# Attention of a four-layer trunk on one core: from one pair of heads at a time to groups of two pairs

## The chip, the cores and the metric

The kernel runs on one core of a Trainium2 chip. The metric is device time in microseconds (us) of one execution. Five engines work beside each other, each in the order of its own queue, and wait for each other by semaphores: PE (TensorE, matmuls and transposes into PSUM), DVE (VectorE), ACT (ScalarE), POOL (GpSimd) and SP, which issues DMAs.

## The reference, cut to what matters

A trunk of one block-sparse attention layer, which at 256 positions is plain causal attention of 16 heads, and one sliding-window layer of 16 query heads on 4 shared key/value heads with a learned sink in the denominator. Each is followed by an output projection and a gated FFN with a convolution over time.

```python
def reference(x, positions, ...):
    for l in range(DEPTH):                       # DEPTH = 2, SEQ = 256, D_MODEL = 1024
        h = rmsnorm(x, attn_norm[l])
        if l < N_A:                              # layer 0: q, k, v of 16 heads of 64
            q, k, v = jnp.split(h @ w_qkv_a[l], 3, axis=-1)
            ...
            o = moba_attention(to_bhsd(q), to_bhsd(k), to_bhsd(heads(v, N_HEADS)))
        else:                                    # layer 1: window of 128, sinks, 4 kv heads
            ...
            o = swa_sink_attention(to_bhsd(q), shared_k, shared_v, sinks_b[i])
        x = x + o.transpose(0, 2, 1, 3).reshape(B_, S_, N_HEADS * HEAD_DIM) @ w_o
        x = x + conv_ffn(rmsnorm(x, ffn_norm[l]), w_up[l], conv_w[l], conv_b[l], w_down[l])
    return rmsnorm(x, final_norm)
```

## The kernel before, in words

Every product in the weights goes as three fp32r matmuls on a high and a low part of each factor (hi·hi, hi·lo, lo·hi). ACT makes the high part of a weight unit (`wh`, L157), DVE the low part (`wl`, L160); a unit is 128x2048 and four are held at once, so the fifth may be written only after PE has read the first for the last time.

Attention takes the 16 heads as 8 pairs. For pair j:

- `score(j)`: three matmuls (L401 to L403) give the first 128 queries of both heads from a block-diagonal key tile `kd`, on all 128 rows of the array. Then six matmuls (L407) of 64 rows each give the second 128 queries, head e from rows 64e to 64e+63; the two heads of a pair can run side by side.
- softmax of each head: `masked` (DVE, L416), `exps` (ACT, L426, with a sink L429), `norm` (DVE L435, L437, L444 and ACT L442). It needs no PE.
- `probs_T(j)`: six transposes (L456), copied from PSUM by DVE (L464) and ACT (L462).
- `values(j)`: four fp32 matmuls (L477) that write 64 columns of the array each, again two heads side by side; each is recorded twice, once for each of two passes. The result is copied as a high part by ACT (L483) and a low part by DVE (L484) into the tile that the output projection reads.

Between these pieces `fill(ns)` takes other PE work from `filler`: the projections of the next q and k groups (L317 to L319) and, at the end, units of the output projection `Down` (L524, L525, L529). `Down` has four units of weights; unit i reads the values of pairs 2i and 2i+1. Two of its units are in the filler, the other two are done by `finish`, by blocks of 128 positions b and halves of the features n; `add` brings each (b, n) into the residual `xr`, and `feats` transposes it (L264) for the FFN, whose first matmuls are L612 to L614.

PSUM has eight banks under three tags: four `acc`, two `u`, two `t`. Steps off PE are put off with `chain` on a clock of estimated PE time. From `manual.close()` on, that is from the first score on, a scheduler of the framework decides the order on each engine from dependencies and priorities, so neighbouring pieces are interleaved there.

In this text a stretch is a run of PE instructions in one shape of the array: *full* (128 rows, 128 columns: projections, L401 to L403, transposes), *row* (64 rows, L407) or *column* (64 columns, L477).

Of the kernel before, what the change touches and what calls it, by code (L numbers as in the profile page):

```python
# [60 lines left out]
def trunk(ctx: ExitStack, tc, x, xw, pos, cpk, fin, sinks, w, out):  # L61
# [32 lines left out]
    def f(ap):  # L94
        return ap.bitcast(F32)

    def blk(b):
        return slice(b * P, (b + 1) * P)
# [279 lines left out]
    def attention(qk, ready, filler, lead, rate, msk, vcol, sink):  # L378

        oT = []  # L380
        budget = [0.0]
# [8 lines left out]

        def score(j):
            g, p = divmod(j, 2)
            while g not in qk:
                next(filler)
            require("qk", g)
            qh, ql, kh_, kl_, kcol, diag = qk[g]
            kc = kcol(p)
            dh, dl = diag(p)
            sa, sb = bank("u"), bank("u")
            o = sa[:, :S]  # L400
            nc.tensor.matmul(o, qh[:, p, blk(0)], dh, start=True, stop=False)  # L401
            nc.tensor.matmul(o, qh[:, p, blk(0)], dl, start=False, stop=False)
            nc.tensor.matmul(o, ql[:, p, blk(0)], dh, start=False, stop=True)  # L403
            for k, (q_, k_) in enumerate(((qh, kh_), (qh, kl_), (ql, kh_))):
                for e, o in enumerate((sa[:, S:], sb[:, :S])):
                    r = slice(e * HD, (e + 1) * HD)
                    nc.tensor.matmul(o, q_[r, p, blk(1)], k_[r, kc], start=(k == 0), stop=(k == 2))  # L407
            tick(640)
            pr = [row3() for _ in range(2)]
            st = wk.tile([P, 4, 4], F32, tag="hst", name=nm("hst"), bufs=4)  # L410

            def masked(e):
                h = 2 * j + e
                src = (sa[:, e * P:(e + 1) * P], sb[:, :S] if e else sa[:, S:])
                for qb in range(NB):
                    nc.vector.tensor_tensor_reduce(out=pr[e][:, qb * P:3 * P] if qb else pr[e][:, :P], in0=src[qb],  # L416
                                                   in1=msk if qb else msk[:, P:], scale=-0.125,
                                                   scalar=nsink[:, h:h + 1] if sink else 3e38, op0=ALU.add, op1=ALU.min,
                                                   accum_out=st[:, 0, 2 * e + qb:2 * e + qb + 1])
# [25 lines left out]

            chain(("sm", j), (200.0, lambda: masked(0)), (400.0, lambda: exps(0)), (600.0, lambda: norm(0)))
            chain(("sm", j), (300.0, lambda: masked(1)), (600.0, lambda: exps(1)), (600.0, lambda: norm(1)))
            return pr

# [19 lines left out]

        def values(j, pT):  # L470

            require("pT", j)
            ov = bank("t")[:, :S]
            for kb in range(NB):
                for e in range(2):
                    o = ov[e * HD:(e + 1) * HD]
                    nc.tensor.matmul(o[:, P:] if kb else o, v_sb[kb][:, vcol(2 * j + e)], pT[e][:, S:] if kb else pT[e][:, :S],  # L477
                                     start=(kb == 0), stop=(kb == 1))
            tick(640)
            if j % 2 == 0:  # L480
                pend[0] = quad()
            hi, lo = pend[0][:, j % 2], pend[0][:, 2 + j % 2]
            chain(("o", j // 2), (200.0, lambda: nc.scalar.activation(hi, ov, AF.Copy)),  # L483
                  (400.0, lambda: nc.vector.tensor_tensor(out=lo, in0=ov, in1=f(hi), op=ALU.subtract)))  # L484
            oT.append((hi, lo))

        ready(oT)
        state, pend = {}, [None]

        fill(lead)  # L490
        manual.close()
        state[0] = score(0)
        n_p = NH // 2
        for j in range(n_p):
            if j + 1 < n_p:
                state[j + 1] = score(j + 1)
            fill(rate(j) * 0.5)
            state[j] = probs_T(j, state[j])
            fill(rate(j) * (1-0.5))
            values(j, state.pop(j))  # L500
        for _ in filler:
# [3 lines left out]
    class Down:  # L505
# [33 lines left out]

        def finish(self, i0, after, tail=None):  # L540

# [5 lines left out]

            for b in range(NB):
                for n in range(2):
# [333 lines left out]
    def filler_a():  # L883
        yield from qk_group(1, U_QK[1])
        yield from qk_group(2, U_QK[2])
        yield from v_half(1, U_V1)
        yield from qk_group(3, U_QK[3])
        yield from o_down[0].units(0, 2)

    def ready_a(oT):  # L890
        o_down.append(Down(U_OA, 4, oT, lambda i: require("o", i)))

    attention(qk, ready_a, filler_a(), 8000.0, lambda h: 7500.0 if h < 6 else 5000.0, mask, lambda h: h, False)
    nc.gpsimd.affine_select(out=mask[:, :P], in_=mask[:, :P], compare_op=ALU.is_gt, fill=NEG, base=0,
# [10 lines left out]

    o_down[0].finish(2, after_a)
    kT_h = new_hT()
# [41 lines left out]
    def filler_b():  # L949
        for g in range(1, 4):  # L950
            yield from q_group(g)
        yield from o_down[0].units(0, 2)

    def ready_b(oT):
        o_down.append(Down(U_OB, 4, oT, lambda i: require("o", i)))

    attention(qk, ready_b, filler_b(), 5500.0, lambda h: 3000.0 if h<4 else 700.0, mask, lambda h: 2 * (h // 8) + h % 2, True)

# [8 lines left out]

    o_down[0].finish(2, after_b)

# [133 lines left out]
```

## Time and profile before

| | |
|---|---|
| median of 3 runs | 585.7 us (585.28 to 585.92) |
| profiled execution, its own time | 585.75 us |
| its span, first to last instruction | 583.8 us |
| PE busy / PEld busy | 574.1 us / 507.1 us |
| DVE / ACT / POOL busy | 432.2 / 381.8 / 105.7 us |
| DMA | 100.99 MB, mean 173 GB/s |

About 2 us of the time lie outside the span. PE is recorded busy nearly all the time; its matmuls overlap, so the distance from the start of one matmul to the start of the next tells more than busy time does. PEld is the loading of the stationary operand, which can run beside a matmul.

### The profile page before, as it was taken

The numbers are of one execution on the slowest core, as the hardware profiler recorded it, in microseconds if no ns is written. First come the engines' busy times: TensorE is split into PE (matmuls) and PEld (weight loads), VectorE is DVE, ScalarE is ACT, GpSimd is POOL, SyncE is SP. The second block draws the span as 40 slices with busy tenths as digits, with TensorE's granted clock in tenths as the row PEclk, the third lists the DMA queues.
The fourth block names the chain that finished last, engine by engine and source line by source line (L and its number), as shares of the span: only waits on it lengthen the run. The fifth ranks groups of instructions, "written<-read, shape, count | busy, mean of one in ns | idle before, by whom it ended". The sixth has DMA issues, their size and how long they took to land.

```text
span 583.8 us, 10178 instructions
## 1 busy us (share of the span) xinstructions
PE 574.1 (98%) x3858; PEld 507.1 (87%) x3858; DVE 432.2 (74%) x929; ACT 381.8 (65%) x768; POOL 105.7 (18%) x124
## 2 busy tenths in 40 slices
PE   8999999999999999999999999999999999999995
PEld 7877777789999999988888977679999999988884
DVE  6697667589977777677569778669987676777814
ACT  6888777579566565666459588758765665656513
POOL 7241001011222322221003000000222223232003
PEclk9999999999999999999999999999999999999999
DMA  8964334314654454547744522143364535446701
GB/s 326 359 265 145 145 144 149 140 60 158 217 198 165 168 194 148 204 153 291 285 144 153 209 74 74 72 145 145 120 241 154 209 145 190 172 163 234 288 0 72
DMA packets 15455, 100.99 MB, mean 173 GB/s; under 512 B 1968, under 2 KB 2096, under 8 KB 3888
## 3 DMA queue, kind: packets, MB, share of 16 engines
q1 hardware_dynamic: 15120, 100.09, 47.0%
q8 instruction: 30, 0.49, 0.3%
q10 hardware_dynamic: 288, 0.26, 0.1%
q14 instruction: 17, 0.14, 0.1%
HBM read 99.30 MB, written 1.05 MB: 172 GB/s over the span
## 4 chain that ended last, share of the span: by engine, by line
PE 60%; DVE 15%; ACT 8%; POOL 6%; issue 5%; DMA 3%; POOLq 0%; SPq 0%; DVEq 0%; ACTq 0%
PE acc L524 9%; PE acc L529 9%; PE acc L525 9%; POOL m L656 6%; DVE m L651 4%; DVE m L649 4%; DVE wl L160 4%; PE acc L317 4%; PE acc L318 4%; PE acc L319 3%; ACT m L645 3%; PE t L477 3%; DMA wr<-in_w 3%; PE t L456 2%; PE u L407 2%
## 5 line engine op out<-in xcount | busy, mean ns | idle before, releaser
L160 DVE TENSOR_TENSOR wl<-wr,wh 128x1024 fp32r<-128x1024 f32 (+1 forms) x200 | 218.9, 1115 | 32.5 <-ACT wh L157 32.2
L157 ACT ACTIVATE wh<-wr 128x1024 fp32r<-128x1024 f32 (+1 forms) x200 | 187.9, 971 | 30.8 <-PE acc L529 17.9
L656 POOL TENSOR_TENSOR m<-m,m 128x256 f32<-128x256 f32 x44 | 66.3, 1507 | 206.7 <-DVE m L651 178.2
L524 PE MATMUL acc<-wh,q 128*128 128x512 f32 x238 | 94.4, 397 | 0.0
L525 PE MATMUL acc<-wl,q 128*128 128x512 f32 x238 | 92.9, 390 | 0.0
L612 PE MATMUL u<-q,wh 128*128 128x256 f32 x320 | 88.4, 277 | 0.0
L613 PE MATMUL u<-q,wh 128*128 128x256 f32 x320 | 88.0, 275 | 0.0
L614 PE MATMUL u<-q,wl 128*128 128x256 f32 x320 | 88.0, 275 | 0.0
L612 PE MATMUL t<-q,wh 128*128 128x256 f32 x288 | 79.4, 276 | 0.7 <-DVE m L651 0.7
L613 PE MATMUL t<-q,wh 128*128 128x256 f32 x288 | 79.2, 275 | 0.0
L614 PE MATMUL t<-q,wl 128*128 128x256 f32 x288 | 79.2, 275 | 0.0
L529 PE MATMUL acc<-wh,q 128*128 128x512 f32 x238 | 79.0, 392 | 0.0
L660 ACT ACTIVATE q<-m 128x256 fp32r<-128x256 f32 x44 | 18.4, 418 | 81.4 <-POOL m L656 81.4
L613 PEld LDWEIGHTS u<-q,wh 128*128 128x128 f32 x320 | 60.1, 188 | 0.0
L614 PEld LDWEIGHTS u<-q,wl 128*128 128x128 f32 x320 | 60.1, 188 | 0.0
L612 PEld LDWEIGHTS u<-q,wh 128*128 128x128 f32 x320 | 59.9, 188 | 0.2
L317 PE MATMUL acc<-wh,q 128*128 128x512 f32 (+1 forms) x160 | 57.2, 358 | 0.0
L318 PE MATMUL acc<-wl,q 128*128 128x512 f32 (+1 forms) x160 | 56.0, 350 | 0.0
L319 PE MATMUL acc<-wh,q 128*128 128x512 f32 (+1 forms) x160 | 55.9, 349 | 0.0
L612 PEld LDWEIGHTS t<-q,wh 128*128 128x128 f32 x288 | 54.1, 188 | 1.0 <-ACT wh L157 0.5
L613 PEld LDWEIGHTS t<-q,wh 128*128 128x128 f32 x288 | 54.1, 188 | 0.0
L614 PEld LDWEIGHTS t<-q,wl 128*128 128x128 f32 x288 | 54.0, 188 | 0.0
(156 smaller groups left out, 1040.3 us busy)
## 6 DMA issues: line engine op xcount, KB each, us to landing
wr<-in_w SPq DMA_DIRECT2D x90, 1024.0 KB, 4.8
first<-in_xw SPq DMA_DIRECT2D x5, 384.0 KB, 5.7
xr<-in_x SPq DMA_DIRECT2D x2, 512.0 KB, 8.6
first<-in_xw SPq DMA_DIRECT2D x1, 768.0 KB, 7.1
out<-m SPq DMA_DIRECT2D x3, 256.0 KB, 2.1
fin_t<-in_fin SPq DMA_DIRECT2D x1, 512.0 KB, 5.7
first<-in_xw SPq DMA_DIRECT2D x1, 388.0 KB, 3.5
out<-m ACTq DMA_DIRECT2D x1, 256.0 KB, 2.1
```

The source lines that it names most:

```text
L157: nc.scalar.activation(wq[i][0][:, c], raws[i][:, c], AF.Copy)
L160: nc.vector.tensor_tensor(out=wq[i][1][:, c], in0=raws[i][:, c], in1=f(wq[i][0][:, c]), op=ALU.subtract)
L317: nc.tensor.matmul(o, xh[:, blk(b)], wh, start=(c == 0), stop=False)
L318: nc.tensor.matmul(o, xh[:, blk(b)], wl, start=False, stop=False)
L319: nc.tensor.matmul(o, xl[:, blk(b)], wh, start=False, stop=(c == KC - 1))
L524: nc.tensor.matmul(o, ph[:, blk(b)], hi[:, s_], start=first, stop=False)
L525: nc.tensor.matmul(o, ph[:, blk(b)], lo[:, s_], start=False, stop=False)
L529: nc.tensor.matmul(o, pl[:, blk(b)], hi[:, s_], start=False, stop=end)
L612: nc.tensor.matmul(o, hi[:, s_], xh, start=(c == 0), stop=False)
L613: nc.tensor.matmul(o, hi[:, s_], xl, start=False, stop=False)
L614: nc.tensor.matmul(o, lo[:, s_], xh, start=False, stop=(c == KC - 1))
L656: nc.gpsimd.tensor_tensor(out=h, in0=gs, in1=t[1], op=ALU.mult)
```

## The change: groups of two pairs

`score(j)` becomes `scores(g)`, which makes the scores of pairs 2g and 2g+1: six block-diagonal matmuls into a bank of their own (tag `acc`, or `t` once `Down` holds all four `acc`), then twelve row matmuls into the two `u` banks. `values(g)` does both pairs of a group into one `t` bank and copies it with one ACT and one DVE instruction of 512 columns. The loop emits `values(g)` right behind `scores(g + 1)`. Three of the four units of `Down` are now in the filler, and `finish` does the last one with the feature half outside and the position block inside (`by_half`). The leads and fill rates are new numbers, and the four heads of a group start their softmax 700 ns apart on the estimated clock.

```diff
-        def score(j):
-            g, p = divmod(j, 2)
+        def scores(g):
             ...
-            sa, sb = bank("u"), bank("u")
-            o = sa[:, :S]
-            nc.tensor.matmul(o, qh[:, p, blk(0)], dh, start=True, stop=False)
...
+            sd, sa, sb = bank("t" if o_down[0].acc else "acc"), bank("u"), bank("u")
+            for p in range(2):
+                dh, dl = diag(p)
+                o = sd[:, p * S:(p + 1) * S]
+                nc.tensor.matmul(o, qh[:, p, blk(0)], dh, start=True, stop=False)
+                nc.tensor.matmul(o, qh[:, p, blk(0)], dl, start=False, stop=False)
+                nc.tensor.matmul(o, ql[:, p, blk(0)], dh, start=False, stop=True)
+            for p in range(2):
+                for k, (q_, k_) in enumerate(((qh, kh_), (qh, kl_), (ql, kh_))):
+                    for e, o in enumerate((sa, sb)):
+                        r = slice(e * HD, (e + 1) * HD)
+                        nc.tensor.matmul(o[:, p * S:(p + 1) * S], q_[r, p, blk(1)], k_[r, kcol(p)],
+                                         start=(k == 0), stop=(k == 2))
+            tick(1600)
+            return [softmax(2 * g + p, p, sd, (sa, sb)) for p in range(2)]
...
-            chain(("sm", j), (200.0, lambda: masked(0)), (400.0, lambda: exps(0)), (600.0, lambda: norm(0)))
-            chain(("sm", j), (300.0, lambda: masked(1)), (600.0, lambda: exps(1)), (600.0, lambda: norm(1)))
+            for e in range(2):
+                chain(("sm", j), (200.0 + 700.0 * (2 * p + e), lambda e=e: masked(e)), (500.0, lambda e=e: exps(e)),
+                      (900.0, lambda e=e: norm(e)))
...
+        def values(g, pT):
+
+            ov = bank("t")
+            for p in range(2):
+                j = 2 * g + p
+                require("pT", j)
...
+            q = quad()
+            hi, lo = q[:, 0:2], q[:, 2:4]
+            ov = ov.rearrange("p (j t) -> p j t", j=2)
+            chain(("o", g), (200.0, lambda: nc.scalar.activation(hi, ov, AF.Copy)),
+                  (600.0, lambda: nc.vector.tensor_tensor(out=lo, in0=ov, in1=f(hi), op=ALU.subtract)))
+            oT.extend((hi[:, p], lo[:, p]) for p in range(2))
...
-        state[0] = score(0)
-        n_p = NH // 2
-        for j in range(n_p):
-            if j + 1 < n_p:
-                state[j + 1] = score(j + 1)
-            fill(rate(j) * 0.5)
-            state[j] = probs_T(j, state[j])
-            fill(rate(j) * (1-0.5))
-            values(j, state.pop(j))
+        n_g = NH // 4
+        state = scores(0)
+        for g in range(n_g):
+            pT = []
+            for p in range(2):
+                fill(rate(g)[p])
+                pT.append(probs_T(2 * g + p, state[p]))
+            fill(rate(g)[2])
+            if g + 1 < n_g:
+                state = scores(g + 1)
+            values(g, pT)
...
+            if by_half:
+                for n in range(2):
+                    for b in range(NB):
+                        for i in range(i0, self.n_u):
+                            unit(i, b, n)
+                        self.add(b, n, after)
...
-        yield from o_down[0].units(0, 2)
+        yield from o_down[0].units(0, 3)
...
-    o_down[0].finish(2, after_b)
+    o_down[0].finish(3, after_b, by_half=True)
```

How the order moves, at three places. First PE in the first attention: pair 1's values (written to `t_743`), pair 3's scores (`u_754`, `u_755`) and what the scheduler put between them, before:

```order
L477 MATMUL t_743<-m_62_706,v_101 64x256
L477 MATMUL t_743<-m_64_712,v_101 64x256
...
L477 MATMUL t_743<-m_64_712,v_102 64x128
L401 MATMUL u_754<-kd_270,q_379 128x256
L402 MATMUL u_754<-kd_270,q_379 128x256
L403 MATMUL u_754<-kd_270,q_380 128x256
L407 MATMUL u_754<-q_379 128x256
L407 MATMUL u_755<-q_379 128x256
L358 MATMUL t_748<-ident,m_65_718 128x128 x4
L407 MATMUL u_754<-q_380,q_379 128x256
```

The same engine after the change, at the scores of group 1 (`acc_690`, `u_691`, `u_692`) and the values of group 0 (`t_724`); L486 is the values' line now, L402 to L404 and L409 the scores':

```order
L404 MATMUL acc_690<-kd_270,q_380 128x256
L409 MATMUL u_691<-q_379 128x256
L409 MATMUL u_692<-q_379 128x256
...
L409 MATMUL u_692<-q_379,q_380 128x256
L486 MATMUL t_724<-m_48_612,v_101 64x256
...
L486 MATMUL t_724<-m_56_664,v_102 64x128
L358 MATMUL t_738<-ident,m_57_681 128x128 x4
```

Twelve row matmuls and eight column matmuls now stand in one piece each, one behind the other; before, four full transposes stood inside the scores and three full matmuls between values and scores. Second, PE at the last stretch of the second attention, behind the values: `t_4361` are the last values before, and `q_4238` and `q_4347` the values of groups 2 and 3 that `Down` reads:

```order
L477 MATMUL t_4361<-m_458_4359,v_102 64x128
L525 MATMUL acc_4119<-wl_3769,q_4087 128x512
L529 MATMUL acc_4118<-wh_3768,q_4087 128x512
L529 MATMUL acc_4119<-wh_3768,q_4087 128x512
L524 MATMUL acc_4116<-wh_3949,q_4238 128x512
...
L525 MATMUL acc_4117<-wl_3950,q_4238 128x512
L529 MATMUL acc_4117<-wh_3949,q_4238 128x512
L524 MATMUL acc_4116<-wh_4130,q_4347 128x512
```

After the change, the values of group 2 (`t_4285`, copied into `q_4300`) and the matmuls of `Down` (now L533, L534, L538) behind them:

```order
L486 MATMUL t_4285<-m_422_4247,v_101 64x256
L486 MATMUL t_4285<-m_420_4241,v_102 64x128
L486 MATMUL t_4285<-m_422_4247,v_102 64x128
L533 MATMUL acc_4070<-wh_3894,q_4300 128x512
L534 MATMUL acc_4070<-wl_3895,q_4300 128x512
```

Fifteen matmuls on earlier values stood between the last values and their first reader; now the reader of a group's values stands directly behind them. Third, ACT at the same stretch after the change: `wh_4309` is the weight unit whose buffer the last matmul ahead of the stretch gives back, `m_426` and `m_427` hold the first two heads of group 3, L432 and L435 are the exps' lines and L492 the copy of the values:

```order
L157 ACTIVATE wh_4309<-wr_3957 128x512 x4
L432 ACTIVATE m_426_4279,hst_4281<-m_426_4279,hst_4281 128x128
L432 ACTIVATE m_427_4280,hst_4281<-m_427_4280,hst_4281 128x128
L432 ACTIVATE m_426_4279,hst_4281<-m_426_4279,hst_4281 128x256
L435 ACTIVATE hst_4281<-hst_4281,sink_t 128x2
L432 ACTIVATE m_427_4280,hst_4281<-m_427_4280,hst_4281 128x256
L492 ACTIVATE q_4300<-t_4285 128x512
```

And before, ACT at the last values (`t_4361`, copied into `q_4347`):

```order
L442 ACTIVATE m_447_4303<-m_447_4303,hst_4304 128x256
L483 ACTIVATE q_4347<-t_4334 128x256
L157 ACTIVATE wh_4374<-wr_3872 128x1024 x2
L462 ACTIVATE m_458_4359<-t_4354 128x384
L483 ACTIVATE q_4347<-t_4361 128x256
L157 ACTIVATE wh_4410<-wr_4024 128x512 x4
```

The copy of the values stands behind four pieces of a weight unit and two heads' exps now; before, the four pieces stood behind it.

## Rows read from the trace of the kernel before

**Rows 1.** The page: busy time and share by engine; granted clock in 40 slices.
```profile
PE 574.1 (98%) x3858; PEld 507.1 (87%) x3858; DVE 432.2 (74%) x929; ACT 381.8 (65%) x768; POOL 105.7 (18%) x124
PEclk9999999999999999999999999999999999999999
```

**Rows 2.** Two windows: length, PE, PEld, DVE, ACT, POOL busy, clock, DMA.
```profile
38.00:110.00 72.00, 71.98 (x405) 55.64 (x404) 52.67 (x159) 54.06 (x129) 7.12 (x13) 1.00 0.44 159
...
334.00:386.00 52.00, 51.96 (x324) 37.80 (x323) 39.19 (x158) 41.99 (x131) 0.00 (x0) 1.00 0.24 82
```

**Rows 3.** Timeline of PE, one pair in the first attention: start, length, what.
```profile
72.78 0.39 PE L319 MATMUL acc<-wh,q 128*128 128x512 f32 x1
73.10 0.87 PE L477 MATMUL t<-m,v 128*64 128x256 f32 x8
73.90 0.39 PE L401 MATMUL u<-kd,q 128*128 128x256 f32 x1
74.12 0.28 PE L402 MATMUL u<-kd,q 128*128 128x256 f32 x1
74.24 0.28 PE L403 MATMUL u<-kd,q 128*128 128x256 f32 x1
74.45 0.38 PE L407 MATMUL u<-q 64*128 64x256 f32 x2
...
75.00 0.50 PE L317 MATMUL acc<-wh,q 128*128 128x512 f32 x1
75.33 0.39 PE L318 MATMUL acc<-wl,q 128*128 128x512 f32 x1
75.56 0.39 PE L319 MATMUL acc<-wh,q 128*128 128x512 f32 x1
```

**Rows 4.** Timeline of PE, second attention: values, then scores, in pieces.
```profile
341.61 0.65 PE L477 MATMUL t<-m,v 128*64 128x256 f32 x2
342.18 0.39 PE L318 MATMUL acc<-wl,q 128*128 128x256 f32 x1
342.50 0.86 PE L477 MATMUL t<-m,v 128*64 128x256 f32 x6
343.29 0.39 PE L319 MATMUL acc<-wh,q 128*128 128x256 f32 x1
...
344.64 0.38 PE L407 MATMUL u<-q,q 64*128 64x256 f32 x1
344.95 0.44 PE L358 MATMUL t<-ident,m 128*128 128x128 f32 x2
```

**Rows 5.** Timeline of ACT, second attention: exps of one head, then norms.
```profile
338.33 0.39 ACT L426 ACTIVATE m<-m,hst 128x128 f32<-128x128 f32 x1
...
339.21 0.28 ACT L429 ACTIVATE hst<-hst,sink_t 128x2 f32<-128x2 f32 x1
339.40 1.69 ACT L442 ACTIVATE m<-m,hst 128x256 f32<-128x256 f32 x4
```

**Rows 6.** Timeline of DVE, second attention: masked scores, starts of two heads.
```profile
336.21 0.35 DVE L416 CUSTOM_DVE_ANT_0 m<-u,mask,nsink 128x128 f32<-128x128 f32 x1
...
336.89 0.35 DVE L416 CUSTOM_DVE_ANT_0 m<-u,mask,nsink 128x128 f32<-128x128 f32 x1
```

**Rows 7.** Groups of ACT instructions by form: copies from PSUM (512 columns, 384).
```profile
L369 ACT ACTIVATE q<-t 128x512 fp32r<-128x512 f32 x8 | 4.7, 590 | 4.4 <-PE t L358 4.3
L462 ACT ACTIVATE m<-t 128x384 f32<-128x384 f32 x16 | 7.8, 486 | 6.2 <-PE t L456 6.0
```

**Rows 8.** Timeline of ACT, second attention: copy of values; a weight unit.
```profile
343.40 0.39 ACT L483 ACTIVATE q<-t 128x256 fp32r<-128x256 f32 x1 [0.80 <-PE t L477]
...
383.23 2.20 ACT L157 ACTIVATE wh<-wr 128x512 fp32r<-128x512 f32 x4 [0.51 <-PE acc L529]
```

**Rows 9.** Timeline of ACT behind the second attention: square and gains of two blocks.
```profile
389.47 0.63 ACT L294 ACTIVATE m<-xr 128x512 f32<-128x512 f32 x1 [0.63 <-DVE xr L588]
...
390.10 2.29 ACT L276 ACTIVATE y<-t,cp 128x128 f32<-128x128 f32 x8
```

More of the change, by code (lines that the diff above doesn't have):

```diff
@@ L396, in score, with softmax @@
             qh, ql, kh_, kl_, kcol, diag = qk[g]
-            kc = kcol(p)
-            dh, dl = diag(p)
-            sa, sb = bank("u"), bank("u")
-            o = sa[:, :S]
-            nc.tensor.matmul(o, qh[:, p, blk(0)], dh, start=True, stop=False)
[L402 to L408, printed above, removed]
+            sd, sa, sb = bank("t" if o_down[0].acc else "acc"), bank("u"), bank("u")
[13 more added lines that the diff above has]
+            return [softmax(2 * g + p, p, sd, (sa, sb)) for p in range(2)]
+        def softmax(j, p, sd, sab):
             pr = [row3() for _ in range(2)]
@@ L413, in masked @@
                 h = 2 * j + e
-                src = (sa[:, e * P:(e + 1) * P], sb[:, :S] if e else sa[:, S:])
+                src = (sd[:, (2 * p + e) * P:(2 * p + e + 1) * P], sab[e][:, p * S:(p + 1) * S])
                 for qb in range(NB):
@@ L468, in probs_T @@
             return out_
[L470 to L485, printed above, removed]
+        def values(g, pT):
[3 more added lines that the diff above has]
+                require("pT", j)
+                for kb in range(NB):
+                    for e in range(2):
+                        o = ov[e * HD:(e + 1) * HD, p * S:(p + 1) * S]
+                        nc.tensor.matmul(o[:, P:] if kb else o, v_sb[kb][:, vcol(2 * j + e)],
+                                         pT[p][e][:, S:] if kb else pT[p][e][:, :S], start=(kb == 0), stop=(kb == 1))
+            tick(1600)
+            q = quad()
[4 more added lines that the diff above has]
+            oT.extend((hi[:, p], lo[:, p]) for p in range(2))
@@ L487, in attention @@
         ready(oT)
-        state, pend = {}, [None]
         fill(lead)
         manual.close()
-        state[0] = score(0)
-        n_p = NH // 2
-        for j in range(n_p):
-            if j + 1 < n_p:
-                state[j + 1] = score(j + 1)
-            fill(rate(j) * 0.5)
-            state[j] = probs_T(j, state[j])
-            fill(rate(j) * (1-0.5))
-            values(j, state.pop(j))
+        n_g = NH // 4
[9 more added lines that the diff above has]
+            values(g, pT)
@@ L538, in units, with finish @@
                 used(self.u + i)
-        def finish(self, i0, after, tail=None):
+        def finish(self, i0, after, tail=None, by_half=False):
             last = self.n_u - 1
@@ L546, in unit @@
                     self.mm(i, k, b, [(n, slice(0, 512))])
-            for b in range(NB):
+            if by_half:
[4 more added lines that the diff above has]
+                        self.add(b, n, after)
+            for b in () if by_half else range(NB):
                 for n in range(2):
@@ L887, in filler_a @@
         yield from qk_group(3, U_QK[3])
-        yield from o_down[0].units(0, 2)
+        yield from o_down[0].units(0, 3)
     def ready_a(oT):
         o_down.append(Down(U_OA, 4, oT, lambda i: require("o", i)))
-    attention(qk, ready_a, filler_a(), 8000.0, lambda h: 7500.0 if h < 6 else 5000.0, mask, lambda h: h, False)
+    attention(qk, ready_a, filler_a(), 8000.0, lambda g: (7000.0, 3500.0, 2000.0) if g < 3 else (5500.0, 2500.0, 1800.0), mask, lambda h: h, False)
     nc.gpsimd.affine_select(out=mask[:, :P], in_=mask[:, :P], compare_op=ALU.is_gt, fill=NEG, base=0,
@@ L904, in after_a @@
         feats(b, n, [(hT, G_FFN[0])], ("x", b, n), y)
-    o_down[0].finish(2, after_a)
+    o_down[0].finish(3, after_a, by_half=True)
     kT_h = new_hT()
@@ L951, in filler_b @@
             yield from q_group(g)
-        yield from o_down[0].units(0, 2)
+        yield from o_down[0].units(0, 3)
     def ready_b(oT):
         o_down.append(Down(U_OB, 4, oT, lambda i: require("o", i)))
-    attention(qk, ready_b, filler_b(), 5500.0, lambda h: 3000.0 if h<4 else 700.0, mask, lambda h: 2 * (h // 8) + h % 2, True)
+    attention(qk, ready_b, filler_b(), 5500.0, lambda g: (3200.0, 2000.0, 1300.0), mask, lambda h: 2 * (h // 8) + h % 2, True)
     hT = new_hT()
```

## The prediction, as it was made before the result was known

> **What bounds the kernel now.** I read the page first. PE is recorded busy for 574.1 of 583.8 us, and its granted clock is 1.00 in all slices, the upper of its two levels (2.4 GHz), so no time is to be had from the clock [rows 1]. Then the windows of the two attentions: PE is busy in 71.98 of 72 us and in 51.96 of 52 us, DVE and ACT in 54 and 42 us or less [rows 2]. PE waits for nobody there that shows. But busy is not work, so I read the timeline of PE for one pair and looked at the distances between starts [rows 3]. Inside a run of full matmuls a 512-column matmul follows the one before it after 0.23 us (75.33 to 75.56) and a 256-column one after 0.12 us (74.12 to 74.24). Where the shape of the array changes, the distances grow twice. On leaving a shape: 0.32 in place of 0.23 us into the column shape (72.78 to 73.10), 0.21 in place of 0.12 us into the row shape (74.24 to 74.45). And again behind the first matmul in the new shape: 0.33 in place of 0.23 us (75.00 to 75.33), 0.22 in place of 0.12 us (73.90 to 74.12). Since no wait is recorded, this is time of PE itself: about 0.1 us for leaving and 0.1 us for the first matmul, **0.20 us for a switch** into full or row. In the second attention the scheduler also cuts stretches into single matmuls, and then a pair that would run side by side runs one after the other [rows 4].
>
> **The change, part by part: what it removes.** I counted shapes in the built order of PE. Before there are 91 switches (44 into full, 25 into row, 22 into column), after it 28 (11, 9, 8). The second attention alone goes from 55 to 15, the first from 36 to 13. The 49 fewer into full and row at 0.20 us are 9.8 us. The price into the column shape is not isolated by a row: at least the 0.09 us of leaving, at most 0.20 us as elsewhere. I take the middle, 0.14 us: 14 fewer make 2.0 us (1.3 to 2.8). Together 11.8 us.
>
> The Trainium skill, TensorEngine Tiling (Array Packing), Key Properties, says that changing the tiling mode, not just the tile, drains TensorE. The trace agrees with the drain (the 0.09 us of leaving) but charges a second 0.1 us that the drain alone doesn't contain; by the drain alone 63 switches would give back 5.7 us. The skill's TensorE: Matmul & The Clock Gate, LDWEIGHTS, puts a weight load at columns / 1.2 ns, so 107 ns for 128 and 53 ns for 64 columns, which would be the second charge if the load can't run ahead of the switch; by it a column switch would cost 0.14 us and the sum would be the same 11.8 us.
>
> Cut stretches: one cut value pair takes 0.57 us for its first two records (341.61 to 342.18) and 0.79 us for the other six (342.50 to 343.29) [rows 4], where the uncut eight take 0.80 us (73.10 to 73.90) [rows 3]. Of the 0.57 us some 0.15 us are that switch, already counted; 0.42 us remain. The order of before has six such cuts, all in the second attention, the order after none: 2.5 us. A score matmul that stands alone takes 0.31 us with its switch (344.64 to 344.95) [rows 4], 0.11 us without it; four slots are lost so: 0.4 us. The removed sum is **14.7 us**, 4.4 of it in the first attention and 10.3 in the second.
>
> **What it adds or moves.** PE does the same matmuls and transposes. The third unit of `Down`, 24 matmuls of 0.23 us, is 5.5 us that move from behind the attention into it: no cost in itself, but less cover behind it. The values' copies are half as many and twice as wide: one of 512 columns is 0.59 us [rows 7] for two of 0.39 us [rows 8]; ACT and DVE gain about a microsecond that they don't need. DMAs, their queue on SP and POOL's work are the same; weights are still prepared up to four units ahead.
>
> So the cost is in new waits of PE, which I sum along the order after the change. Times are from the start of a stretch of scores and values: six full matmuls 0.7 us, row part 6 x 0.11 + 0.2 = 0.9 us, values 2 x 0.62 + 0.14 = 1.4 us (0.62 is the uncut 0.80 without its switch charges); the stretch is 3.0 us long.
>
> - Last stretch of the second attention. The first matmul behind it reads the values just made. ACT can't begin the four pieces of the weight unit until the last matmul ahead of the stretch has ended, some 0.35 us into it; they take 2.20 us [rows 8]. Then, ahead of the copy, come the exps of two heads without the second sink, 2 x 1.07 (338.33 to 339.40) less 0.19 us (339.21 to 339.40), about 1.9 us [rows 5], and the copy, 0.59 us [rows 7]. That is 5.0 us, against 3.1 us of PE's own: a wait of 1.9 us. Queued behind it on ACT are the rest of group 3's exps and all its norms, which the last transposes wait for.
> - Behind the last values of each attention the last unit of `Down` reads them at once; ACT starts a copy 0.04 us after the recorded end of the values (342.50 + 0.86 to 343.40) [rows 4, 8] and takes 0.59 us. With the tail of the matmul, 0.8 us each, and in the first attention one more piece of a weight unit, 0.55 us, may stand ahead. I take 1.7 us for both. Before, fifteen matmuls on older values covered this.
> - Those last values themselves wait for the last copy of probabilities, 0.49 us [rows 7]: 0.3 us in the second attention. In the first, twelve matmuls (2.7 us) lie between.
> - The first groups of the second attention. `masked` takes 0.68 us a head (336.21 to 336.89) [rows 6], exps 1.07 us (338.33 to 339.40), a norm 0.4 us [rows 5]. The first transposes come 5.5 us after the start of group 0's scores, the first head's norm ends at about 5.9 us since weight parts and table loads stand between: with the later heads 0.7 us of waits, in group 1 another 0.3 us. In group 2 and in the first attention's groups, between whose scores and transposes 24 or more 512-column matmuls (5.5 us) lie, I find none.
> - Starts of the FFNs. The four blocks (b, n) now end 1.4 us apart (six matmuls) where the last two were 2.7 us apart and the first two were long done. ACT has 0.63 us of square and 2.29 / 2 us of gains for each [rows 9], 1.8 us in all. The first FFN matmul needs two blocks, and then the two broadcasts of the norm follow late: 0.5 us each, 1.0 us.
>
> Visible waits: 1.9 + 1.7 + 0.3 + 1.0 + 1.0 = 5.9 us. I add 1 us for what such a reading of a queue misses: 6.9 us. **Sum: 585.75 - 14.7 + 6.9 = 578.0 us.** It is made on the profiled execution, which took 585.75 us, 0.05 above the median of the runs; no correction.
>
> **The rivals.** (a) *The order keeps PE full, as it does now.* Rows 2 speak for it: with ACT at 42 of 52 us no wait shows. Against it: the reader behind the values has no other work ahead of it, so about 2 us stay. 585.75 - 14.7 + 2 = 573 us. (b) *The second charge isn't given back.* If the extra 0.1 us behind a switch were a cost of the narrow matmuls and came in a long stretch too, only leaving counts: 63 x 0.09 + 2.9 = 8.6 us, less 6.9: 584.1 us. Against it: the second charge stands behind the first *full* matmul too (75.00 to 75.33) [rows 3]. The drain of the skill's page, taken alone, is this rival. (c) *Slower: ACT's chain of four heads becomes the bound.* Per group ACT then has 4 x 1.07 of exps, 4 x 0.4 of norms, a copy of 0.59, two copies of probabilities of 0.49 and a weight unit of 2.2 us [rows 5, 7, 8]: 9.6 us in series, of which all but the last copies must be done between scores and values. PE's work per group in the second attention falls from 13 to some 11.8 us (52 - 10.3 + 5.5, by four), so there are only 2 us of slack, and DVE's parts lie between ACT's. If each of the eight groups waits 2.5 us, that is 20 us: 585.75 - 14.7 + 20 = 591 us. It decides from 1.8 us of waits per group on. Against it: in the first attention a group has 18 us of PE work, so four of the eight groups have no reason to wait, and 3.7 us in each of the other four would be needed.
>
> The skill's TensorEngine Tiling (Array Packing), PSUM Bottleneck, warns that a faster TensorE doesn't empty PSUM any faster and that ACT and DVE may become the bottleneck; rival (c) is its form here, and the 42 of 52 us of ACT are the nearest that the trace shows of it.
>
> **How the numbers follow.** About 0.2% (1.2 us) is what a measurement of this kernel can tell from no change. Chances: my forecast, waits between 4 and 11 us, 575 to 582 us: 0.58. Rival (a), 571 to 575 us: 0.20. Rival (b) or waits of 11 to 13.5 us, 582 to 584.6 us: 0.09. Waits that just eat the gain, 584.6 to 586.9 us: 0.05. Rival (c), above: 0.08. So faster 0.87, same 0.05, slower 0.08. The range leaves out about 0.08 at the bottom and some 0.12 at the top: 572.0 to 583.5 us. Its ends are also those of the unknown prices: with 0.20 us for a column switch and 2 us of waits 572.2 us; with 0.09 us and 11 us of waits 582.8 us.
>
> **What would show it.** Right: PE's distances inside a stretch of twelve and eight matmuls without a switch charge (about 0.8 and 1.4 us for them), the second attention shorter by some 6 us and the first by 2 to 3 us (work that moved into them set aside), and a gap of PE of about 2 us behind the last stretch of the second attention, released by ACT's copy of the values. Wrong: gaps of PE ahead of the transposes in most groups (rival c), a second charge inside a long stretch (rival b), or no gap behind the stretches (rival a). What would make the prediction wrong above all is the size of the waits: they are read from an order, and one late instruction on ACT shifts all behind it.

## The result, and the profile after

The kernel after takes 578.09 us (median of 4 runs, 577.80 to 578.59), the kernel before 585.81 us beside it: ratio 0.987, 95% interval 0.9858 to 0.9882, **1.3% faster**. The forecast was 578.0 us. The profiled execution took 578.59 us, its span is 576.7 us.

The page's PE line and clock of the kernel after, which answer to [rows 1]:

```profile
PE 561.9 (97%) x3858; PEld 505.3 (88%) x3858; DVE 429.2 (74%) x921; ACT 379.3 (66%) x760; POOL 106.3 (18%) x124
...
PEclk9999999999999999999999999999999999999998
```

PE runs the same 3858 matmuls in 12.2 us less of recorded busy time, at the same clock, but the span is only 7.1 us shorter: the rest are waits that show now. Windows of the kernel after (columns as in [rows 2]):

```profile
38.00:106.00 68.00, 68.00 (x402) 55.59 (x401) 52.65 (x156) 53.76 (x126) 6.95 (x13) 1.00 0.48 169
...
329.00:367.00 38.00, 37.59 (x286) 31.91 (x286) 32.23 (x125) 34.31 (x101) 0.00 (x0) 1.00 0.29 101
367.00:381.00 14.00, 11.34 (x78) 8.70 (x75) 10.90 (x40) 10.87 (x34) 0.00 (x0) 1.00 0.39 143
```

In the first attention PE still waits for nobody that shows up to 106 us (a wait of 0.8 us behind its last values comes at 111 us); in the second it idles 3 us, nearly all of it in 14 us at the end. Busy time hides the rest, so I cut the span at four starts of PE: first score of each attention (L401 before, L402 after), and the 41st matmul of each FFN's first kind (L612, L627), by which both kernels have done all transposes and broadcasts of the FFN's start.

| us | lead-in | first attention to FFN | FFN to second attention | second attention to FFN | FFN to the end |
|---|---|---|---|---|---|
| before | 38.30 | 99.24 | 193.65 | 79.23 | 173.4 |
| after | 38.61 | 95.83 | 194.32 | 73.92 | 174.0 |
| difference | +0.3 | **-3.4** | **+0.7** | **-5.3** | **+0.6** |

The attentions give 8.7 us, and the FFNs, whose code is untouched, take 1.3 us back. The lead-in, up to the first score, lies between 37.7 and 39.8 us in all the kernels below, so they are compared by the other four pieces, each from the one profiled execution of its kernel.

PE at a stretch of the first attention after the change, to be held against [rows 3]:

```profile
56.59 0.28 PE L402 MATMUL acc<-kd,q 128*128 128x256 f32 x1
...
57.18 0.29 PE L404 MATMUL acc<-kd,q 128*128 128x256 f32 x1
57.39 0.39 PE L409 MATMUL u<-q 64*128 64x256 f32 x2
57.62 0.40 PE L409 MATMUL u<-q,q 64*128 64x256 f32 x4
57.85 0.28 PE L409 MATMUL u<-q 64*128 64x256 f32 x2
57.97 0.40 PE L409 MATMUL u<-q,q 64*128 64x256 f32 x4
58.30 1.52 PE L486 MATMUL t<-m,v 128*64 128x256 f32 x16
59.75 0.66 PE L358 MATMUL t<-ident,m 128*128 128x128 f32 x4
```

Both charges stand once for each shape: 0.21 us on leaving full (57.18 to 57.39), 0.23 us for the first two row matmuls (57.39 to 57.62) where two later ones take 0.12 us (57.85 to 57.97). Twelve row matmuls take 0.91 us (57.39 to 58.30) and the values of two pairs 1.45 us (58.30 to 59.75), where the sum had 0.9 and 1.4.

The waits of PE from the second attention to the FFN behind it (time waited, times, longest):

```profile
PE acc L533 <- ACT q L492: 2.3, 2, 1.6
PE t L486 <- DVE m L471: 0.3, 1, 0.3
PE t L715 <- DVE m L719: 0.3, 1, 0.3
PE t L463 <- ACT m L448: 0.2, 1, 0.2
PE t L358 <- DVE hst L441: 0.2, 1, 0.2
```

The two largest are those of `Down` for values that have just been copied. PE at the last stretch:

```profile
365.08 0.61 PE L538 MATMUL acc<-wh,q 128*128 128x512 f32 x2
365.54 0.28 PE L402 MATMUL t<-kd,q 128*128 128x256 f32 x1
...
366.34 0.97 PE L409 MATMUL u<-q,q 64*128 64x256 f32 x12
367.24 1.52 PE L486 MATMUL t<-m,v 128*64 128x256 f32 x16
370.41 0.50 PE L533 MATMUL acc<-wh,q 128*128 128x512 f32 x1 [1.64 <-ACT q L492]
```

And ACT there:

```profile
365.74 2.20 ACT L157 ACTIVATE wh<-wr 128x512 fp32r<-128x512 f32 x4 [0.88 <-PE acc L538]
367.83 0.39 ACT L432 ACTIVATE m<-m,hst 128x128 f32<-128x128 f32 x1
...
369.28 0.49 ACT L432 ACTIVATE m<-m,hst 128x256 f32<-128x256 f32 x1
...
369.77 0.58 ACT L492 ACTIVATE q<-t 128x512 fp32r<-128x512 f32 x1
```

ACT stands idle 0.88 us until PE gives back the weight buffer, makes four pieces of a weight unit (2.1 us), then the exps of two heads (1.94 us), then the copy. The values were done at about 368.7, and PE waits 1.6 us for a copy that needs 0.58 (1.7 us by the distance of the starts, which is how the sums of waits below are counted).

### The profile page after: what moved, and what is told of

Its sections match the earlier page's. It is cut to its first block, busy times and chain, and to the rows that moved or that the text cites. A ratio compares the mean times of both kernels' runs of the same rounds, so it can differ in the third digit from the quotient of the medians.

```text
span 576.7 us, 10181 instructions
## 1 busy us (share of the span) xinstructions
PE 561.9 (97%) x3858; PEld 505.3 (88%) x3858; DVE 429.2 (74%) x921; ACT 379.3 (66%) x760; POOL 106.3 (18%) x124
## 4 chain that ended last, share of the span: by engine, by line
PE 60%; DVE 12%; ACT 12%; POOL 6%; issue 5%; DMA 4%; POOLq 0%; SPq 0%; DVEq 0%; ACTq 0%
PE acc L533 9%; PE acc L534 9%; PE acc L538 9%; POOL m L671 5%; DVE m L666 4%; ACT m L660 3%; DVE m L664 3%; PE acc L317 3%; PE acc L318 3%; PE acc L319 3%; DMA wr<-in_w 3%; PE t L627 3%; PE t L628 3%; PE t L629 2%; DVE wl L160 2%
## 5 line engine op out<-in xcount | busy, mean ns | idle before, releaser
L533 PE MATMUL acc<-wh,q 128*128 128x512 f32 x238 | 94.4, 397 | 3.1 <-ACT q L492 3.1
L534 PE MATMUL acc<-wl,q 128*128 128x512 f32 x238 | 92.9, 390 | 0.0
L627 PE MATMUL u<-q,wh 128*128 128x256 f32 x320 | 88.6, 277 | 0.7 <-DVE m L666 0.7
L627 PE MATMUL t<-q,wh 128*128 128x256 f32 x288 | 79.6, 276 | 0.7 <-DVE m L666 0.7
L538 PE MATMUL acc<-wh,q 128*128 128x512 f32 x238 | 77.2, 390 | 0.0
L675 ACT ACTIVATE q<-m 128x256 fp32r<-128x256 f32 x44 | 18.4, 418 | 85.9 <-POOL m L671 85.9
L627 PEld LDWEIGHTS u<-q,wh 128*128 128x128 f32 x320 | 60.1, 188 | 1.3 <-ACT wh L157 1.0
L533 PEld LDWEIGHTS acc<-wh,q 128*128 128x128 f32 x238 | 44.7, 188 | 12.6 <-ACT q L492 3.9
L627 PEld LDWEIGHTS t<-q,wh 128*128 128x128 f32 x288 | 54.1, 188 | 1.2 <-ACT wh L157 0.5
```

What stands on the lines that cost most here:

```text
L533: nc.tensor.matmul(o, ph[:, blk(b)], hi[:, s_], start=first, stop=False)
L534: nc.tensor.matmul(o, ph[:, blk(b)], lo[:, s_], start=False, stop=False)
L538: nc.tensor.matmul(o, pl[:, blk(b)], hi[:, s_], start=False, stop=end)
L627: nc.tensor.matmul(o, hi[:, s_], xh, start=(c == 0), stop=False)
```

## The experiments

Each kernel was timed beside the kernel before on the same chip. The kernel after was not timed again there; its ratio of 0.987 makes it 577.7 us in the first four and 577.8 us in the next four.

**1. Scores pair by pair inside the stretch.** Sixteen switches more than the kernel after.

```diff
                 nc.tensor.matmul(o, ql[:, p, blk(0)], dh, start=False, stop=True)
-            for p in range(2):
                 for k, (q_, k_) in enumerate(((qh, kh_), (qh, kl_), (ql, kh_))):
```

> The kernel after, but inside a stretch the scores go pair by pair (three full, six row, three full, six row) in place of six full and twelve row matmuls; everything else is as in the kernel after. The built order has 44 switches of the array's shape in place of 28: eight more from row into full and eight more from full into row. My theory (a switch costs about 0.2 us because of the leaving and of the first matmul behind it): 16 x 0.20 = 3.2 us more than the kernel after, so about 581.3 us. Rival, only leaving costs (0.09 us): 1.4 us more, 579.5 us. Rival, switches cost nothing and the gain came from elsewhere: 578.1 us.

Measured: 579.34 us, ratio 0.9902 (0.9886 to 0.9918), 1.6 us over the kernel after: half of what I expected, and next to what the rival said. The trace decides between them. PE at the same place:

```profile
57.99 0.28 PE L402 MATMUL acc<-kd,q 128*128 128x256 f32 x1
...
58.44 0.39 PE L408 MATMUL u<-q 64*128 64x256 f32 x2
58.66 0.40 PE L408 MATMUL u<-q,q 64*128 64x256 f32 x4
58.99 0.39 PE L402 MATMUL acc<-kd,q 128*128 128x256 f32 x1
59.21 0.28 PE L403 MATMUL acc<-kd,q 128*128 128x256 f32 x1
...
60.09 1.52 PE L485 MATMUL t<-m,v 128*64 128x256 f32 x16
```

The scores take 2.10 us (57.99 to 60.09) where the kernel after takes 1.71 (56.59 to 58.30): two switches for 0.39 us, **0.20 us each**, with a first matmul behind each that is 0.1 us late again (58.99 to 59.21, where 59.21 to 59.33 is the usual 0.12). The first attention is 1.40 us longer for its eight switches (97.23 us). The second is 0.30 us *shorter* (73.62) with eight more, since its waits fall by 1.7 us, from 4.7 to 3.0: the wait behind the last stretch from 1.64 to 0.99, those of the first groups from 1.1 to 0.2. Behind the last stretch PE comes some 0.4 us later because of two switches, and ACT is further on by that much. In the first groups more has changed than the switches: the scheduler built another order, in which the first transposes of group 0 stand 7.1 us behind the start of its scores in place of 5.7. So the price is right; how much of the 1.7 us the switches alone would have hidden, this run does not separate. What it refutes is my expectation of the total, not the price.

**2. The last stretch earlier.** One piece of `Down` moves behind it.

```diff
-    attention(..., lambda g: (3200.0, 2000.0, 1300.0), ...)
+    attention(..., lambda g: (3200.0, 2000.0, 1300.0 if g < 2 else 0.0), ...)
```

> The kernel after, but in groups 2 and 3 of the second attention the third fill is 0 in place of 1300 ns, so that one piece of Down (six matmuls, 1.4 us) moves from ahead of the stretch with the scores of group 3 to behind it; ACT's four pieces of a weight unit then come behind the copy of the values. My theory: PE's wait of 1.8 us behind that stretch is set by ACT's queue ahead of that copy and goes; the built order has two switches more (0.4 us): 1.4 us less than the kernel after, about 576.7 us. Rival, the softmax of group 3 is late by itself and the wait only moves to its transposes: 578 to 578.5 us.

Measured: 577.11 us, ratio 0.9858 (0.9842 to 0.9875), 0.6 us under the kernel after, which the two intervals alone do not tell apart. PE there:

```profile
366.23 1.52 PE L486 MATMUL t<-m,v 128*64 128x256 f32 x16
367.68 0.50 PE L533 MATMUL acc<-wh,q 128*128 128x512 f32 x1
...
369.15 0.39 PE L533 MATMUL acc<-wh,q 128*128 128x512 f32 x1
```

And ACT:

```profile
367.97 0.57 ACT L492 ACTIVATE q<-t 128x512 fp32r<-128x512 f32 x1
...
369.81 0.62 ACT L157 ACTIVATE wh<-wr 128x512 fp32r<-128x512 f32 x1
```

The wait is gone, and so are those behind and ahead of the last values: the second attention takes 71.30 us, 2.6 us less. The edit does two things at once, though. ACT's pieces of the weight unit now stand behind the copy (369.81), and six matmuls on older values (the first starts at 367.68, before the copy does) now stand between the values and their reader (369.15). The copy ends at 368.54. My estimate from these rows: with the four pieces (2.1 us) still ahead of it, it would have ended at about 370.6 us and the six matmuls would not have covered it; with the pieces gone but no six matmuls, some 0.7 us of wait would be left. So the queue of ACT ahead of the copy is the larger part of the cause, and missing cover the rest; the two were not run apart. But the last piece takes 175.43 us, 1.4 us more. PE's waits between 425 and 570 us, in the second FFN:

```profile
PE t L627 <- DVE m L666: 0.8, 3, 0.3
PE u L627 <- DVE m L666: 0.6, 2, 0.3
```

Five of them, where the kernel after has two and the kernel before one. (0.3 us is the idle time on record; by the distance of the starts each costs some 0.5 us.) Experiments 4, 6 and 7 are about these.

**3. The part on `Down` undone.**

```diff
-        yield from o_down[0].units(0, 3)
+        yield from o_down[0].units(0, 2)
...
-    o_down[0].finish(3, after_b, by_half=True)
+    o_down[0].finish(2, after_b)
```

(in both attentions)

> The kernel after with the part on Down undone: two of its units in the filler, and the end in the old order (blocks outside). The built order puts 13 and 4 matmuls on older values behind the last values of the two attentions. My theory: the waits behind the last values (0.96 and 0.87 us) and the late second broadcast of the norm at both FFN starts (0.5 us each) go, 2.8 us; the wait of 1.8 us behind the last stretch stays, and the transposes of group 3 come sooner behind it, which may cost 1 us: 575.3 to 576.5 us. Rival, the third unit in the filler is what covers the softmax of the last group: 579 us or more. Rival, Down's part is neutral: 578.1 us.

Measured: 576.46 us, ratio 0.9847 (0.9828 to 0.9866), 1.3 us under the kernel after, as my theory had it; but its four runs lie from 575.17 to 577.44 us and the interval overlaps that of the kernel after, so the total is not clear of the noise. The pieces of the profiled execution (575.72 us) say more. The first attention is 1.3 us shorter (94.53 us), the first FFN 0.6 (193.74); in the second attention the waits behind the last values and of the broadcast go, but a new one of 1.1 us ahead of the FFN's transposes comes (73.70 us, 0.2 less); the last piece is 0.2 us shorter. Together 2.3 us. By these pieces the groups without this part bring more than the whole change. The edit undoes the third unit and the new order of the end together, so it does not say which of the two costs.

**4. The estimated clock as before.**

```diff
-            tick(1600)
+            tick(1280)
```

(in `scores` and `values`)

> The kernel after, but scores and values of a group each advance the estimated clock by 1280 ns in place of 1600, which is what two pairs advanced it by in the kernel before. Due times of softmax steps and of weight units move a little; the built order of the second attention has two switches fewer. My theory: two switches give 0.4 us, and the two new waits of about 0.5 us in each FFN (PE for a bank that DVE's taps still read) come from the phase of the weight units on that clock and go back to one: together 1.4 us less than the kernel after, 576.7 us. Rival, the FFN's waits have nothing to do with that clock: 0.4 us less, 577.7 us.

Measured: 577.69 us, ratio 0.9869 (0.9854 to 0.9883): what the rival said, no difference that the times show (the second attention is 0.2 us shorter for its two switches). The waits at the FFNs' ends stand where they stood (two of 0.5 us in each). **My theory of them fell:** they are not the phase of that clock.

**5. Values cut, as the scheduler had cut them.** In groups 0 to 2 of the first attention.

```diff
                         nc.tensor.matmul(o[:, P:] if kb else o, v_sb[kb][:, vcol(2 * j + e)],
                                          ...)
+                        if (p, kb, e) == (0, 0, 0) and g < 3 and not sink:
+                            budget[0] -= next(filler)
```

> The kernel after, but in groups 0 to 2 of the first attention three to six full matmuls of the filler are put between the first value matmul and the other seven, as the scheduler did in the kernel before; the fill behind is shorter by as much. Three cuts: six switches more. My theory (a cut also costs 0.42 us because the two matmuls that would run side by side run one after the other): 3 x (2 x 0.18 + 0.42) = 2.3 us more than the kernel after. Rival, a cut is only its two switches: 1.1 us more. Rival, neither: no difference.

Measured: 580.2 us, ratio 0.9909 (0.9895 to 0.9923), 2.4 us over the kernel after; the first attention takes 98.10 us, 2.27 us more, the others are the same to 0.2 us. PE at one cut:

```profile
57.44 0.65 PE L486 MATMUL t<-m,v 128*64 128x256 f32 x2
58.01 0.50 PE L317 MATMUL acc<-wh,q 128*128 128x512 f32 x1
...
58.90 1.51 PE L486 MATMUL t<-m,v 128*64 128x256 f32 x14
60.34 0.66 PE L358 MATMUL t<-ident,m 128*128 128x128 f32 x4
```

From 57.44 to 60.34 are 2.90 us, 0.69 of them the three full matmuls, so 2.21 us for values that take 1.45 uncut: 0.76 us a cut, three times 2.3 us. This is the term of the prediction (0.42 us and two switches), shown by itself.

**6. The taps of the FFN in another order.** The taps are the three terms of the convolution over time; ACT makes one and DVE adds the other two, for each half of a unit. DVE and ACT in a late unit of the kernel after's second FFN, first DVE:

```profile
453.18 0.48 DVE L664 SCALAR_TENSOR_TENSOR m<-t,cp,m 128x255 f32<-128x255 f32 x1 [0.48 <-ACT m L660]
...
454.48 1.22 DVE L160 TENSOR_TENSOR wl<-wr,wh 128x1024 fp32r<-128x1024 f32 x1
455.62 0.47 DVE L666 SCALAR_TENSOR_TENSOR m<-t,cp,m 128x254 f32<-128x254 f32 x1
...
459.22 0.48 DVE L664 SCALAR_TENSOR_TENSOR m<-u,cp,m 128x255 f32<-128x255 f32 x1 [0.49 <-ACT m L660]
```

And ACT:

```profile
452.14 1.01 ACT L660 ACTIVATE m<-t,cp 128x256 f32<-128x256 f32 x2
...
457.85 0.42 ACT L675 ACTIVATE q<-m 128x256 fp32r<-128x256 f32 x1 [2.21 <-POOL m L671]
458.18 1.01 ACT L660 ACTIVATE m<-u,cp 128x256 f32<-128x256 f32 x2
```

A unit comes every 6.04 us there (453.18 to 459.22), while 48 matmuls of PE take 48 x 0.1133 = 5.44 us. In a loop ACT's taps release DVE's, the last of them POOL's product, that ACT's copy L675, and behind it in ACT's queue stand the next unit's taps. I worked out for each unit its lag, the time from the start of its last matmul to the end of DVE's last tap: in the kernel after 10.3 us at unit 5 of the second FFN, 0.6 more with each unit, up to 18.6 us. There PE's next unit needs a bank that DVE's taps still read, and PE waits 0.5 us for each unit that is left. In the kernel before it was 9.8 us at unit 5, in experiment 2 it was 11.8.

The loop itself is no work of the change. In the kernel before, DVE's first taps of two units in the first FFN:

```profile
229.62 0.48 DVE L649 SCALAR_TENSOR_TENSOR m<-u,cp,m 128x255 f32<-128x255 f32 x1 [0.49 <-ACT m L645]
...
235.67 0.48 DVE L649 SCALAR_TENSOR_TENSOR m<-t,cp,m 128x255 f32<-128x255 f32 x1 [0.48 <-ACT m L645]
```

They are 6.05 us apart, and the lag ends at 18.6 us there too. The kernels differ in the lag with which an FFN starts, and so in how many units are left when it reaches 18.6.

```diff
                 for j in range(2):
                     nc.vector.scalar_tensor_tensor(out=t[j][:, 1:], ..., scalar=w1[j], ...)
+                for j in range(2):
                     nc.vector.scalar_tensor_tensor(out=t[j][:, 2:], ..., scalar=w0[j], ...)
```

> The kernel after, but DVE's four taps of a FFN unit are written as first tap of both halves, then second tap of both halves, in place of half by half, so that no low part of a weight unit lies between them in DVE's order. Attention is as in the kernel after. In the trace of the kernel after one unit's loop over ACT, DVE and POOL takes 6.04 us where PE takes 5.45, the lag of DVE's last tap behind the unit's last matmul grows by 0.6 us a unit to 18.6 us, and from there PE waits 0.5 us a unit: twice in each FFN (once in each before). My theory: without the 1.22 us in the loop the lag does not grow and the four waits go: 2.0 us less than the kernel after. Rival, the loop is set by something else: no difference.

Measured: 575.62 us, ratio 0.9834 (0.9819 to 0.985), 2.2 us under the kernel after; the attentions are unchanged (95.85 and 73.91 us), the FFN pieces are 1.45 and 1.0 us shorter, and no wait of PE is left at the end of either. DVE now:

```profile
455.40 1.22 DVE L160 TENSOR_TENSOR wl<-wr,wh 128x1024 fp32r<-128x1024 f32 x1 [0.53 <-ACT wh L157]
456.55 0.86 DVE L664 SCALAR_TENSOR_TENSOR m<-u,cp,m 128x255 f32<-128x255 f32 x2
457.33 0.86 DVE L667 SCALAR_TENSOR_TENSOR m<-u,cp,m 128x254 f32<-128x254 f32 x2
```

The waits went, but not as I expected: the weight piece only moved ahead of the taps (455.40 to 461.36, the next unit's, is 5.96 us), and the lag still grows by 0.5 us a unit. It begins lower (9.1 us at unit 5) and ends at 17.4, short of the 18.6 at which PE waits. Why it begins lower is open.

**7. The part on `Down` alone**, in the kernel before.

> The kernel before with the part on Down alone: three units in the filler, the last by feature halves. My theory: in the first attention the last values get a reader close behind them and one more cut (0.6 + 0.8 us of waits, 0.35 + 0.42 us for the cut), and at both FFN starts the second broadcast comes late (0.45 us each): 3 us more than the kernel before, some 588.5 us. Rival, the third unit covers the softmax at the end and gives back as much: no difference. Rival, it is this part and not the groups that makes the kernel after faster: 580 us or less.

Measured: 590.56 us, ratio 1.0086 (1.0072 to 1.0101), 5.1 us *slower* than the kernel before. The first attention is 2.15 us longer, as expected, the second 0.4; the FFNs take 0.5 and 2.3 us more, which I had not expected: PE waits five times at the end of the second, where the lag at unit 5 is 12.1 us. PE's waits from 200 to 250 us, at the end of the first FFN, in this run and then in experiment 3:

```profile
PE t L618 <- DVE m L657: 0.3, 1, 0.3
PE u L618 <- DVE m L657: 0.3, 1, 0.3
```

```profile
PE t L627 <- DVE m L666: 0.3, 1, 0.3
```

So with this part and without the groups the first FFN has the two waits of the kernel after, although PE gained nothing ahead of it; with the groups and without this part it has the one of the kernel before. There the second wait goes with the part on `Down`, not with the faster attention. In the second FFN it is two waits in experiment 3 and five here; what sets the lag there is open.

**8. What the runs point to.** Old `Down` in the first attention, late fill in the second, taps in the new order.

> The kernel after with three edits: in the first attention two units of Down in the filler and its end in the old order; in the second the third fill of groups 2 and 3 is 0; in the FFN the taps in the new order. From the traces so far: 1.3 us less in the first attention, 2.6 us less in the second, and the waits at the ends of the FFNs (1.0 us each in the kernel after, 2.3 us in the second FFN with the late fill) gone: 5.9 us less than the kernel after, about 572 us. If the FFN's loop is set by something else: 2.6 us less, 575.5 us.

Measured: **573.13 us, ratio 0.979 (0.9776 to 0.9804)**, faster than both kernels; 4.7 us under the kernel after where I had 5.9. The attentions came as added up (94.43 and 71.30 us). The last piece is 174.50 us, 1.5 more than in experiment 6: the lag starts at 10.7 us, comes to 18.2, and waits of 0.2, 0.4 and 0.4 us remain, the last of them for DVE's part of a weight unit behind the FFN's loop. With the taps in this order PE waits at a lag of 18.2 already.

**9. The taps in the kernel before.**

> The kernel before with the FFN's taps in the new order alone. Before, PE waits once at the end of each FFN (0.50 and 0.49 us). My theory: they go, 1.0 us less than the kernel before, about 584.4 us; against the kernel after with the same taps the change then gains a good 1 us more than it does with the taps as they are, which is what the FFNs take back. Rival, the new order of the taps helps the kernel after alone: no difference.

Measured: 584.29 us, ratio 0.9982 (0.9973 to 0.9991), 1.1 us under the kernel before. With the taps so in both kernels the change is worth 0.9834 / 0.9982 = 0.985, 8.7 us where it is 7.6 us as they are. By the times this difference of 1 us is within the intervals; by the pieces it is clear: the last piece and the one from FFN to second attention take 366.0 us here and 365.9 us in experiment 6, where the kernel after has 1.3 us more than the kernel before.

## Why the prediction was right

**The removed sum, 14.7 us.** The first attention is 3.4 us shorter with 1.3 us of new waits in it, the second 5.3 us with 4.7 us (each wait is the distance between two starts less what the same two matmuls take without one): 4.7 + 10.0 = 14.7 us, where the prediction had 4.4 and 10.3. This is the difference of the spans with the waits added, so it proves the sum only as far as the waits are all seen. It can be taken directly as well: the distances between the starts of all row and column matmuls, with what the full ones next to them take beyond their distance inside a run and without the waits, add up to 15.7 us before and 10.4 us after in the first attention, 20.8 and 10.8 us in the second. That is 5.3 + 10.0 = 15.3 us; the other 0.6 us went into the full matmuls and transposes between the stretches, which this does not take apart. So the exact 14.7 is partly luck: the first attention's part was 0.9 us too small (and the attention as a whole 3.4 us shorter where the text had 2 to 3), the second's 0.3 us too large.

Its two prices stand by themselves in experiments 1 and 5: 0.20 us a switch (0.175 by the length of the first attention in experiment 1), 0.42 us for a cut beside its two switches. The price into the column shape, taken at 0.14 us as a middle, the trace of the kernel after bears out: on top of the 0.09 us of leaving, the first pair of values at the last stretch takes 0.26 us from its second record to the next pair (367.25 to 367.51), the same pair of the second half 0.21 us (367.95 to 368.16), so 0.05 us more.

**The new waits, 6.9 us.**

| us | predicted | measured |
|---|---|---|
| last stretch of the second attention | 1.9 | 1.7 |
| behind the last values, both attentions | 1.7 | 0.9 + 0.8 |
| last values for their probabilities | 0.3 | 0.4 |
| first groups of the second attention | 1.0 | 1.1 |
| starts of the FFNs | 1.0 | 1.2 |
| what the reading misses | 1.0 | 1.3 at the FFNs' ends, 0.3 lead-in (within its spread) |

Together 7.6 us. The queue of ACT at the last stretch came to pass row by row (pieces 0.2 us into the stretch in place of 0.35, exps 1.94 us for 1.9, copy 0.58 for 0.59), and experiment 2 bears it out as the larger part of that wait. The late broadcasts are in both FFN starts (0.45 us each), on DVE's product of L719, not on ACT's squares and gains alone as the text had it. What the reading missed had a place: the loop of the FFN. That line was a guess which came out near; its mechanism was not in the text, and by experiments 3 and 7 half of it (the first FFN's part) comes with the part on `Down`.

**The rivals.** (a) fell: 6 us of waits stand between the attentions and the FFN starts. (b) fell: inside the long stretch two row matmuls take 0.12 us without a second charge (57.85 to 57.97), and experiment 1 shows that the second charge comes again with each switch that is added. The Trainium skill, TensorEngine Tiling (Array Packing), Key Properties, has a drain at a switch of modes; the trace agrees with it (0.09 us on leaving) and adds the 0.1 us behind it. (c) fell where it was put: no group waits 1.8 us for its softmax, the most are 0.6 us (group 0 of the second attention). Other engines do bound a part of this program, the FFNs, at 6.04 against 5.44 us a unit, but they did so before the change as well: it is not rival (c). The Trainium skill warns under PSUM Bottleneck of the same page that copies out of PSUM may become the bottleneck behind a tiled TensorE; the nearest that this trace shows are PE's three waits for ACT's copy of the values, 0.8, 1.6 and 0.7 us.

**`Down`.** The text held the third unit to be no cost in itself, but less cover behind. The runs have it as a cost, together with the new order of the end: 1.3 us by the times and 2.3 us by the pieces with the groups (experiment 3), and 5.1 us without them (experiment 7), 2.9 us of these in the FFNs, which the text did not have.

## What to carry to other kernels

Distances between starts, not busy time, show what a change of the array's shape costs; count such changes in the built order, price them from one stretch, and then look for the reader that stands directly behind the work that was drawn together, because its copy in another engine's queue becomes the next wait. And compare the parts that the change did not touch: where a loop over the other engines is longer than PE's (6.04 against 5.44 us a unit here, before and after), a small shift at its start comes out as a wait of PE hundreds of matmuls later. The lag, unit by unit, shows it long before PE waits.

## What the runs showed that was not expected

That the loss need not be near its cause: a lag of ACT and DVE that is 1.5 us larger at the start of an FFN (11.8 against 10.3 us at unit 5, experiment 2) costs three more waits of 0.5 us at its end, from some 60 us later on. It is not simply that a faster attention starts the FFN with a larger lag: experiment 7, with a slower attention, has the largest (12.1). And a kernel with eight more switches (some 1.4 us) can have a second attention that is 0.3 us shorter, because its waits shrink by more than that.
